# A two-group streaming encoder layer on one core: the layer-input gate's weight sums beside the first projection, the feed-forward operands in another order, the first residual rows requested early

## The chip, the cores and the metric

The kernel runs on one core of one Trainium2 chip. The metric is the device time of one execution in microseconds (us). A core has a matrix engine (TensorE, PE in the profile), three elementwise engines (VectorE is DVE, ScalarE is ACT, GpSimd is POOL) and SyncE (SP), which here issues all transfers, in order, to one queue that 16 DMA engines work off. Each engine runs its instructions in the order in which they stand, and waits on semaphores for the others.

## What is computed

One encoder layer over 1024 prompt tokens and 8 x 16 sample tokens, that is nine tiles of 128 tokens, of width 1024, all in float32:

```python
h = rmsnorm(x, g_mix)
q_a, k_a, v_a, q_b, k_b, v_b = split_heads(h, w_in)      # 1024 -> 3072
a   = stick_breaking(q_a, k_a, v_a, ...)                 # group A, 8 heads; samples also see a cache
o_b = band_attention(q_b, k_b, v_b, ..., rel_table)      # group B, 8 heads
x = x + concat(rmsnorm(a), rmsnorm(o_b)) @ w_out
h = rmsnorm(x, g_ffn)
x = x + (silu(h @ w_gate) * (h @ w_up)) @ w_down         # 1024 -> 2816 -> 1024
gate = sigmoid(rmsnorm(x, g_ple) @ w_ple_gate)           # 1024 x 1024, the layer-input gate
x = x + gate * (p @ w_ple_proj)
y = rmsnorm(x, g_final)
```

The new keys and values are outputs too. In the gate, the scale `g_ple` belongs to the rows of `w_ple_gate`, so that `g_ple * w_ple_gate` depends on weights alone and can be made at any time before the gate's product.

## The kernel before, in words

**Precision and products.** Each float32 operand is split into a high part (a cast on ACT, line L159, L233 or L1303) and the rest (a subtraction, L105, on DVE or POOL), and each product is three matmuls (`mm3`, L100 to L102). The products of the feed-forward block, of the down projection and of the gate use a scheme of Strassen's kind: seven products of half-size blocks instead of eight. Their operands are sums of blocks, `B11, B21, B22, T1, T2, T3, T4` for the feed-forward block ("forms", 16 KB a partition each, both parts together). The gate's weight sums are `gated[0]` to `gated[6]`, written to device memory and read back by the gate's stage at the end.

**Stages.** First projection with normalization (up to about 330 us), attention, output projection and feed-forward norm (ending about 880 us), gate and up products (to about 1350 us), down projection (1350 to 1580 us), gate and end.

**Who sets the order.** A scheduler orders the instructions of each engine, except within `manual_schedule` blocks and `keep_in_program_order`, where they stay as written. `advance(main, side, ratio, steps)` takes steps from a generator `main` and, by `ratio`, takes steps from a generator `side` between them, so that the side's instructions are written down among the main's. Memory comes from pools on the left and on the right end of a partition; a pool that lies where an earlier one was waits for the last users of what was there.

**First projection.** `qkv` works through `w_in` in chunks of 256 columns (`wraw`, 1 MB a load): the keys of group A (0,1,0) and (0,1,1), then its queries (0,0,0) and (0,0,1), then the rest. Keys: nine matmul tiles of 128x256 a chunk go to `st`, are transposed in threes, split into `sq` (two buffers, `tag="sq"`) and stored in device memory (`kT0h`, `kT0l`, L242). Queries: six tiles of 128x384 a chunk, computed already transposed into two PSUM banks (`ps["o"]`), split from the bank by ACT (L236) and DVE (L237) into the same `sq`, and stored (`qT0h`, `qT0l`). A bank is free when both have read it; an `sq` is free when its stores have landed. `draw` loads rows of the key cache for the attention, and `sk` is the first attention load.

**Gate-up to down.** The forms lie in a row in the order in which they are made, T4, B22, B11, B21, T2, T3, T1, after `h8`. When the last product is done, the down stage's pools lie over them: `sA` (`acth`, `actl`, operands of the down products) over the first two, `sB` (`actr` activations, `wr` weights, `sr` sums) over the others. The last gate-up products read T4, then B22. `raws` loads the first operands, `forms` makes them, `put` splits one. `onto` (L1349) adds each product to the residual rows `x1`, which `fetch_x1` (L1363) loads from `x1d`.

**Down stage.** Five rounds (`d`); in rounds 1 to 4 `gate_sums(d - 1)` makes a quarter of the gate's weight sums: four loads of `w_ple_gate` (L1384, 256 KB each), four scalings on ACT (L1385), four subtractions on POOL (L1393 to L1396) and seven stores (L1389, 256 KB each). Its tiles `q00, q01, q10, q11, t2, t3` have one buffer each.

Of the kernel before, what the change touches and what calls it, by code (L numbers as in the profile page):

```python
# [22 lines left out]
P = 128  # L23
D = 1024
KT = 8
NP = 8
NT = 9
# [12 lines left out]
def tile_hymba_step(  # L40
# [37 lines left out]
    nc = tc.nc  # L78
    V, A, G, T = nc.vector, nc.scalar, nc.gpsimd, nc.tensor
# [141 lines left out]
    gated = [dram.tile([P, 4, 512], F32, name=f"gated{i}") for i in range(7)]  # L221
# [496 lines left out]
    left, right = ExitStack(), ExitStack()  # L718
    ps = {}

    def pool(stack, name, side, bufs=1):
        return stack.enter_context(tc.tile_pool(name=name, bufs=bufs, side=side, reuse_waits="tile"))

    def banks(stack, side, **n):
        for k, m in n.items():
            ps[k] = stack.enter_context(
                tc.tile_pool(name=f"ps_{k}_{len(pool_names)}", bufs=m, space=PSUM, side=side, reuse_waits="tile")
            )
            pool_names.append(k)
# [3 lines left out]
    def advance(main, side, ratio, steps=None):  # L733

        due, n = 0.0, 0
        while steps is None or n < steps:
            if next(main, "end") == "end":
                break
            n += 1
            due += ratio  # L740
            while due >= 1.0:
                due -= 1.0
                next(side, None)
        return n
# [12 lines left out]
    with tc.tile_pool(name="x1", bufs=2, side="right") as xp, tc.manual_schedule(engines=all_engines):  # L757
# [22 lines left out]
        for i in range(4):  # L780
            o = slice(i * 2, i * 2 + 2)
# [7 lines left out]
        for t in range(2, NT):  # L789
# [2 lines left out]
            transposed(ps["t"], rows.pop(0), hT, t)  # L792
            next(project)
    start.close()
    banks(first, "left", t=2, s=1)
    advance(project, None, 0, 36 - (NT - 1))

    for i, g in enumerate((g_out_sb, g_out_cb)):
        nc.sync.dma_start(g_out[:, i * 4 : i * 4 + 4], g.rearrange("o (k p) -> p (o k)", p=P))
# [172 lines left out]
    def form(name):  # L972
        return [fp.tile([P, KT // 2, 512], F32R, name=name + n) for n in "hl"]


    h8 = [fp.tile([P, KT, P], F32R, name="h8" + n) for n in "hl"]
    T4, B22, B11, B21, T2, T3, T1 = [form(n) for n in ("T4", "B22", "B11", "B21", "T2", "T3", "T1")]
    g_row = load_row(xg, g_ffn[0:1, :], "grow")

    def gate_up(i):  # L980
# [170 lines left out]
    with tc.tile_pool(name="ph4b", bufs=2, side="right", reuse_waits="tile") as p4b:  # L1151
# [12 lines left out]
        for i in range(n_chunk):  # L1164
# [28 lines left out]
            d = bank()  # L1193
# [60 lines left out]
        bstack = ExitStack()  # L1254
# [105 lines left out]
    def fetch_x1(ts, half):  # L1360
        for t in ts:
            o = slice(half * 512, half * 512 + 512)
            nc.sync.dma_start(x1[t][:, o], x1d[t * P : (t + 1) * P, o])  # L1363


    with tc.manual_schedule(engines={mybir.EngineType.SP}):
        fetch_x1((0, 1, 2, 3, 8), 0)
        fetch_x1((4, 5, 6, 7), 1)
        fetch_x1((0, 1, 2, 3, 8), 1)
        fetch_x1((4, 5, 6, 7), 0)  # L1370
        ahead = raws(1)

    wq = pool(bstack, "wq", "left")
    g_gate = wq.tile([P, KT], F32, name="g_gate")
    nc.sync.dma_start(g_gate, g_ple.rearrange("o (k p) -> p (o k)", p=P))

    def gate_sums(k):

        q = {}
        for x in range(2):  # L1380
            for y in range(2):
                q[x, y] = wq.tile([P, 512], F32, name=f"q{x}{y}", tag=f"q{x}{y}", bufs=1)
                row = (x * 4 + k) * P
                nc.sync.dma_start(q[x, y], w_ple_gate[0, row : row + P, y * 512 : y * 512 + 512])  # L1384
                A.activation(q[x, y], q[x, y], AF.Copy, scale=g_gate[:, x * 4 + k : x * 4 + k + 1])  # L1385
        t2, t3 = [wq.tile([P, 512], F32, name=nm, tag=nm, bufs=1) for nm in ("t2", "t3")]

        def out(i, v):
            nc.sync.dma_start(gated[i][:, k], v)  # L1389

        for i, v in ((0, q[0, 0]), (1, q[1, 0]), (6, q[1, 1])):
            out(i, v)
        G.tensor_tensor(t3, q[1, 1], q[0, 1], op=ALU.subtract)  # L1393
        G.tensor_tensor(q[0, 1], q[0, 1], q[0, 0], op=ALU.subtract)
        G.tensor_tensor(t2, q[1, 1], q[0, 1], op=ALU.subtract)
        G.tensor_tensor(q[1, 0], q[1, 0], t2, op=ALU.subtract)  # L1396
        for i, v in ((2, t2), (3, t3), (4, q[0, 1]), (5, q[1, 0])):
            out(i, v)

    for d in range(nd):  # L1400
        if d:
            ahead = raws(d + 1) if d + 1 < nd else None
        if ahead is None:
            w_last = sB.tile([P, 2, D], F32, name="wr", tag="wr", bufs=3)
            nc.sync.dma_start(w_last, w_down[0, 2 * nd * 256 :, :].rearrange("(f p) c -> p f c", p=P))
            a_last = []
            for f in range(2):
                a_last.append(sB.tile([P, 2, NT * P], F32, name="actr", tag="actr", bufs=4)[:, 0])
                nc.sync.dma_start(a_last[f], actd[2 * nd][:, f])
        A2, W21, A1, W11, d8 = got  # L1410
        got = next(now)
        for m in range(4):
            b = bank()
            times(b, A2, W21, m)
            onto(m, 0, b)
        m1 = []
        for m in range(4):
            m1.append(tbank())
            times(m1[m], A1, W11, m)
            onto(m, 0, m1[m])  # L1420
        b = bank()
        last_tile(d8, 1, W21, b, True, False)
        last_tile(d8, 0, W11, b, False, True)
        onto(NP, 0, b)
        S2, T2, S1, T1 = got
        got = next(now)
        for m in range(4):
            times(m1[m], S2, T2, m, True)
            if d == 0:
                A.copy(u2[m], m1[m])  # L1430
            else:
                V.tensor_tensor(u2[m], u2[m], m1[m], op=ALU.add)
        m5 = []
        for m in range(4):
            m5.append(bank())
            times(m5[m], S1, T1, m)
            onto(4 + m, 1, m5[m])
        S4, W22, W12 = got
        got = next(now)
        for m in range(4):  # L1440
            times(m5[m], S4, W22, m, True)
            onto(m, 1, m5[m])
        b = bank()
        last_tile(d8, 1, W22, b, True, False)
        last_tile(d8, 0, W12, b, False, True)
        onto(NP, 1, b)
        S3, T3, A4, T4 = got
        if d:
            gate_sums(d - 1)
        if ahead is not None:  # L1450
            now = forms(ahead)
            got = next(now)
        else:
            w_d = ch.parts(w_last, 2, D, 2, V)
            act = []
            for f in range(2):
                hl = act_place(NT * P)
                A.copy(hl[0], a_last[f])
                sub(G, hl[1], a_last[f], hl[0])
                act.append(hl)  # L1460
        m7 = []
        for m in range(4):
            m7.append(tbank())
            times(m7[m], S3, T3, m)
            onto(4 + m, 1, m7[m])
        for m in range(4):
            times(m7[m], A4, T4, m, True)
            onto(4 + m, 0, m7[m])
# [270 lines left out]
```

## Time and profile before

| | |
|---|---|
| median of the runs shown | 1710.83 us (1707.01, 1710.83, 1711.6) |
| profiled execution, its time | 1708.87 us |
| its span in the trace | 1707.0 us (1.87 us lie around it) |
| granted TensorE clock | 0.989 |
| PE busy | 1650.5 us, 97% of the span |
| DVE, ACT, POOL busy | 1083.7, 814.2, 819.5 us |
| moved by DMA | 293.50 MB, 172 GB/s on average |

A time in the rows that follow counts from the start of the span. A row of a timeline has the start, the duration, the engine and line, what is written and read, and in brackets how long the engine had been idle and what ended that. In a row of a tile there are minimum, median and maximum durations in ns. In a row by stretches of time the busy time of each engine stands with the number of its instructions, then the granted clock, the share of time that the DMA engines were busy and GB/s.

### The profile page before, as it was taken

To read this page: it belongs to the slowest core of one execution; us is meant where nothing else is said; L and a number is where in the kernel's file an instruction comes from. 1 tells how busy PE (TensorE), PEld (TensorE's weight loads), DVE (VectorE), ACT (ScalarE), POOL (GpSimd) and SP (SyncE) were. 2 spreads that over 40 slices of the span, in tenths; PEclk is the share of its full clock that TensorE was granted. 3 is DMA by queue.
4 is the path that set the end of the run, shared out by engine and by line. 5 is a ranking of instruction groups with operands and counts; after the bars stand their busy time and mean duration, and the time that the engine had idled before them with its cause. 6 is when DMAs were issued, how large, how long until landed. Compare 5 with 4: busy or idle time off the path is not lost.

```text
span 1707.0 us, 27775 instructions
## 1 busy us (share of the span) xinstructions
PE 1650.5 (97%) x10308; PEld 1422.1 (83%) x10308; DVE 1083.7 (63%) x1702; ACT 814.2 (48%) x1724; POOL 819.5 (48%) x666
## 2 busy tenths in 40 slices
PE   8999999989998999898999999999999999999998
PEld 7998888989996887787878888888888788788887
DVE  6111544369889766754677566666655597798875
ACT  5223545367777877643663333333333244433673
POOL 2313311277356511322565555555555378958763
PEclk9999999999998999999999999999999999999999
DMA  5846888656469985955422222222222697712222
GB/s 193 277 151 218 276 292 296 186 179 173 123 175 275 290 262 163 254 173 173 148 87 96 96 96 96 96 96 96 85 86 89 217 384 255 251 67 114 97 99 100
DMA packets 172810, 293.50 MB, mean 172 GB/s; under 512 B 16641, under 2 KB 96257, under 8 KB 170370
## 3 DMA queue, kind: packets, MB, share of 16 engines
q1 hardware_dynamic: 172674, 291.71, 52.1%
q8 instruction: 82, 1.34, 0.3%
q14 instruction: 54, 0.44, 0.1%
HBM read 204.77 MB, written 86.90 MB: 171 GB/s over the span
## 4 chain that ended last, share of the span: by engine, by line
PE 80%; DVE 6%; DMA 6%; ACT 3%; POOL 3%; issue 2%; SPq 1%; POOLq 0%; DVEq 0%; ACTq 0%
PE ps L1076 25%; PE ps L100 7%; PE ps L101 6%; PE ps L102 6%; PE pt L1344 4%; PE pt L1076 4%; PE ps L1344 3%; PE pt L610 2%; PE pt L405 2%; PE acc L468 2%; DMA v<-sv 2%; DVE keep L114 2%; PE sdec L427 1%; PE po L634 1%; PE S L579 1%
## 5 line engine op out<-in xcount | busy, mean ns | idle before, releaser
L105 POOL TENSOR_TENSOR wlo<-wraw,whi 128x512 fp32r<-128x512 f32 (+1 forms) x123 | 216.4, 1783 | 137.9 <-ACT whi L159 137.9
L100 PE MATMUL ps<-whi,hTh 128*128 128x256 f32 x576 | 168.0, 292 | 1.4 <-ACT st L267 1.4
L101 PE MATMUL ps<-wlo,hTh 128*128 128x256 f32 x576 | 164.5, 286 | 0.0
L102 PE MATMUL ps<-whi,hTl 128*128 128x256 f32 x576 | 164.0, 285 | 0.0
L159 ACT CAST whi<-wraw 128x512 fp32r<-128x512 f32 (+1 forms) x122 | 88.6, 743 | 72.5 <-PE ps L1076 27.5
L100 PEld LDWEIGHTS ps<-whi,hTh 128*128 128x128 f32 x576 | 110.6, 192 | 8.0 <-issue 5.7
L592 POOL TENSOR_TENSOR w<-w,keep 128x127 f32<-128x127 f32 (+4 forms) x64 | 78.5, 1229 | 74.8 <-DVE keep L114 64.6
L102 PEld LDWEIGHTS ps<-whi,hTl 128*128 128x128 f32 x576 | 110.7, 192 | 0.6 <-DVE hTl L105 0.2
L101 PEld LDWEIGHTS ps<-wlo,hTh 128*128 128x128 f32 x576 | 110.8, 192 | 0.2
L614 ACT CAST wth<-pt 128x512 fp32r<-128x512 f32 (+1 forms) x192 | 84.3, 466 | 44.1 <-PE pt L610 43.4
L105 DVE TENSOR_TENSOR wtl<-pt,wth 128x512 fp32r<-128x512 f32 (+1 forms) x192 | 94.1, 512 | 14.8 <-ACT wth L614 14.7
L114 DVE TENSOR_TENSOR_SCAN keep<-keep,zero 128x128 f32<-128x128 f32 (+7 forms) x64 | 101.6, 1588 | 1.7
L610 PE MATMUL pt<-ident,w 128*128 128x128 f32 x528 | 90.1, 284 | 6.7 <-DVE wtl L105 3.1
L610 PEld LDWEIGHTS pt<-ident,w 128*128 128x128 f32 x528 | 63.9, 144 | 20.3 <-DVE wtl L105 5.3
L579 PE MATMUL S<-qk 128*128 128x384 f32 (+2 forms) x192 | 71.9, 376 | 7.3 <-ACT keep L583 5.4
L633 PE MATMUL po<-wth,vk 128*128 128x256 f32 (+1 forms) x304 | 76.8, 284 | 1.2 <-DVE wtl L105 1.2
L105 POOL TENSOR_TENSOR actl<-actr,acth 128x1024 fp32r<-128x1024 f32 (+1 forms) x22 | 60.5, 2751 | 32.2 <-DMA sr<-acts 20.7
L634 PE MATMUL po<-wtl,vk 128*128 128x256 f32 (+1 forms) x304 | 73.5, 285 | 0.0
L406 DVE COPY kT<-pt 128x512 f32<-128x512 f32 x48 | 33.0, 687 | 51.7 <-PE pt L405 47.7
L101 PE MATMUL ps<-hTl,whi 128*128 128x384 f32 x192 | 65.4, 341 | 0.0
L102 PE MATMUL ps<-hTh,wlo 128*128 128x384 f32 x192 | 65.3, 340 | 0.0
L100 PE MATMUL ps<-hTh,whi 128*128 128x384 f32 x192 | 65.2, 339 | 0.0
(448 smaller groups left out, 5291.5 us busy)
## 6 DMA issues: line engine op xcount, KB each, us to landing
draw<-in_cache_sb_k SPq DMA_DIRECT2D x32, 512.0 KB, 6.3
draw<-in_cache_sb_v SPq DMA_DIRECT2D x32, 512.0 KB, 5.5
act<-sg SPq DMA_DIRECT2D x11, 1152.0 KB
actr<-act SPq DMA_DIRECT2D x22, 576.0 KB, 6.3
wraw<-in_w_in SPq DMA_DIRECT2D x11, 1024.0 KB, 9.4
wraw<-in_w_gate SPq DMA_DIRECT2D x11, 1024.0 KB, 5.3
wraw<-in_w_up SPq DMA_DIRECT2D x11, 1024.0 KB, 6.3
v<-sv SPq DMA_DIRECT2D x36, 256.0 KB, 4.5
```

Of the source, the lines that this page charges most:

```text
L100: T.matmul(out, lhsT=ah, rhs=bh, start=start, stop=False)
L101: T.matmul(out, lhsT=ah, rhs=bl, start=False, stop=False)
L102: T.matmul(out, lhsT=al, rhs=bh, start=False, stop=stop)
L105: return eng.tensor_tensor(out, a, hi.bitcast(F32), op=ALU.subtract)
L114: V.tensor_tensor_scan(rev, rev, zero[:, 0:1].to_broadcast([P, n - d]), keep[:, n - d : n - d + 1], op0=ALU.mult, op1=ALU.max)
L159: A.copy(h[:, o], v[:, o])
L579: T.matmul(sc, lhsT=hd["qq"][:, qs], rhs=hd["kkh"][:, kc], start=True, stop=False)
L610: T.transpose(pt[:, (c - c0) * P : (c - c0 + 1) * P], w[:, c * P : (c + 1) * P], ident)
L614: A.copy(wth[:, ks, qs], pv)
L634: T.matmul(dst, lhsT=vs, rhs=wtl[:, kb - base, c0:c1], start=False, stop=(i == nkb - 1))
L1076: T.matmul(out, lhsT=a[x][:, k], rhs=b[y][:, k], start=(not more and k == 0 and n == 0), stop=(k == 3 and n == 2), skip_group_check=more)
L1344: T.matmul(out, lhsT=a[i][:, x, m * P : (m + 1) * P], rhs=b[j][:, x], start=(not more and x == 0 and n == 0), stop=(x == 1 and n == 2), sk ...
```

## The change

It has three parts.

1. `gate_sums` moves from the down stage to the first projection. It becomes a generator with three steps a quarter (loads; scalings, three stores and a subtraction; three subtractions and four stores), runs as `side` of `advance` with a ratio of 0.5, and its tiles come from a pool on the right end of memory, with two buffers each, in the place that the input rows `x` leave. The 16 loads, 16 scalings, 16 subtractions and 28 stores are the same ones.
2. The forms are laid out as B21, T2, B11, T3, T1, T4, B22. `sA` then lies over B21 and T2, and `sB` over the others, of which T4 and B22 are the last.
3. `fetch_x1` for the first halves of rows 0 to 3 is called ahead of the `manual_schedule` block rather than within it.

```diff
@@ after the first tiles of the projection
     start.close()
+    qstack = ExitStack()
+    wq = pool(qstack, "wq", "right", 2)
+    g_gate = wq.tile([P, KT], F32, name="g_gate", bufs=1)
+    nc.sync.dma_start(g_gate, g_ple.rearrange("o (k p) -> p (o k)", p=P))
+
+    def gate_sums(k):
+        q = {}
+        for x in range(2):
+            for y in range(2):
+                q[x, y] = wq.tile([P, 512], F32, name=f"q{x}{y}", tag=f"q{x}{y}")
+                row = (x * 4 + k) * P
+                nc.sync.dma_start(q[x, y], w_ple_gate[0, row : row + P, y * 512 : y * 512 + 512])
+        yield
+        for x, y in q:
+            A.activation(q[x, y], q[x, y], AF.Copy, scale=g_gate[:, x * 4 + k : x * 4 + k + 1])
+        t2, t3 = [wq.tile([P, 512], F32, name=nm, tag=nm) for nm in ("t2", "t3")]
...
+        for i, v in ((0, q[0, 0]), (1, q[1, 0]), (6, q[1, 1])):
+            out(i, v)
+        G.tensor_tensor(t3, q[1, 1], q[0, 1], op=ALU.subtract)
+        yield
+        G.tensor_tensor(q[0, 1], q[0, 1], q[0, 0], op=ALU.subtract)
+        G.tensor_tensor(t2, q[1, 1], q[0, 1], op=ALU.subtract)
+        G.tensor_tensor(q[1, 0], q[1, 0], t2, op=ALU.subtract)
+        for i, v in ((2, t2), (3, t3), (4, q[0, 1]), (5, q[1, 0])):
+            out(i, v)
+        yield
+
     banks(first, "left", t=2, s=1)
-    advance(project, None, 0, 36 - (NT - 1))
+    gate_weights = (x for k in range(4) for x in gate_sums(k))
+    advance(project, gate_weights, 0.5, 36 - (NT - 1))
+    for _ in gate_weights:
+        pass
+    qstack.close()
@@ feed-forward
-    T4, B22, B11, B21, T2, T3, T1 = [form(n) for n in ("T4", "B22", "B11", "B21", "T2", "T3", "T1")]
+    B21, T2, B11, T3, T1, T4, B22 = [form(n) for n in ("B21", "T2", "B11", "T3", "T1", "T4", "B22")]
@@ down
+    fetch_x1((0, 1, 2, 3), 0)
     with tc.manual_schedule(engines={mybir.EngineType.SP}):
-        fetch_x1((0, 1, 2, 3, 8), 0)
+        fetch_x1((8,), 0)
...
-    wq = pool(bstack, "wq", "left")
...
-        if d:
-            gate_sums(d - 1)
```

**The first projection, SP's queue at the change from keys to queries.** Before, from the last four key stores on (names as in the code, with buffer numbers; `sq_980` and `sq_1027` are the same buffer of two):

```order
L242 DMA kT0h_72<-sq_980 128x384
L242 DMA kT0h_72<-sq_989 128x384
L242 DMA kT0l_73<-sq_980 128x384
L242 DMA kT0l_73<-sq_989 128x384
L141 DMA wraw_1182<-in_w_in 128x8x256
L365 DMA sk0_1621<-kT0h_72 128x4x128
L242 DMA qT0h_70<-sq_1027 128x384
L242 DMA qT0l_71<-sq_1027 128x384
```

The same place now (`sq_1028` is what was `sq_980`, `wraw_1255` what was `wraw_1182`; L814 are the stores and L807 the loads of `gate_sums`):

```order
L141 DMA wraw_1255<-in_w_in 128x8x256
L814 DMA gated3_116<-t3_1250 128x512
L807 DMA q10_1392<-in_w_ple_gate 128x512
L814 DMA gated0_113<-q00_1388 128x512
L814 DMA gated4_117<-q01_1179 128x512
L814 DMA gated6_119<-q11_1394 128x512
L814 DMA gated2_115<-t2_1249 128x512
L814 DMA gated1_114<-q10_1181 128x512
L242 DMA kT0h_72<-sq_1028 128x384
L242 DMA kT0l_73<-sq_1028 128x384
L242 DMA kT0h_72<-sq_1037 128x384
L814 DMA gated3_116<-t3_1461 128x512
```

The load of the next weights and seven transfers of `gate_sums` now stand ahead of the first of the last four key stores. The loads `draw`, which stood earlier, now stand behind the first four query stores.

**The same place on POOL and ACT.** POOL now has, from the split of the chunk before on:

```order
L105 TENSOR_TENSOR wlo_193<-wraw_1044,whi_192 128x1024 x2
L818 TENSOR_TENSOR t3_1250<-q11_1183,q01_1179 128x512
L820 TENSOR_TENSOR q01_1179<-q01_1179,q00_1177 128x512
L821 TENSOR_TENSOR t2_1249<-q11_1183,q01_1179 128x512
L818 TENSOR_TENSOR t3_1461<-q11_1394,q01_1390 128x512
```

ACT now has, up to the first query split (before, L233, L233 and L236 stood side by side):

```order
L233 CAST sq_1028<-pt_1024 128x384
L810 ACTIVATE q01_1390<-q01_1390,g_gate_646 128x512
L233 CAST sq_1037<-pt_1033 128x384
L810 ACTIVATE q10_1392<-q10_1392,g_gate_646 128x512
L236 ACTIVATE sq_1075<-ps_1050 128x384
```

Two scalings have come between the splits, and on POOL the four subtractions of a quarter follow the split of `wraw_1044`, where nothing stood before.

**The down stage, POOL in the round that starts about 1450 us.** Before:

```order
L1310 TENSOR_TENSOR t2_15411<-wraw_15133,t2_15411 128x1024
L1393 TENSOR_TENSOR t3_16059<-q11_16055,q01_16049 128x512
L105 TENSOR_TENSOR actl_15584<-sr_15149,acth_15583 128x1024
L1394 TENSOR_TENSOR q01_16049<-q01_16049,q00_16046 128x512
L105 TENSOR_TENSOR actl_15653<-actr_15138,acth_15652 128x1024
L1395 TENSOR_TENSOR t2_16058<-q11_16055,q01_16049 128x512
L1310 TENSOR_TENSOR wr_15141<-wraw_15133,wr_15141 128x2x512
L1396 TENSOR_TENSOR q10_16052<-q10_16052,t2_16058 128x512
```

The same place now:

```order
L1346 TENSOR_TENSOR t2_15487<-wraw_15234,t2_15487 128x1024
L105 TENSOR_TENSOR actl_15660<-sr_15250,acth_15659 128x1024
L105 TENSOR_TENSOR actl_15729<-actr_15239,acth_15728 128x1024
L1346 TENSOR_TENSOR wr_15242<-wraw_15234,wr_15242 128x2x512
L105 TENSOR_TENSOR actl_15735<-actr_15236,acth_15734 128x1024
```

The subtractions are gone from between the splits.

**SP at the start of down.** The rows here read as before but for line numbers and buffer numbers: the last activations, then the residual rows 0 to 3 and 8:

```order
L1285 DMA act10_100<-sg_14540 128x2304
L1399 DMA x1_0_14885<-x1d_89 128x512
L1399 DMA x1_1_14886<-x1d_89 128x512
L1399 DMA x1_2_14887<-x1d_89 128x512
L1399 DMA x1_3_14888<-x1d_89 128x512
L1399 DMA x1_8_14893<-x1d_89 128x512
```

Nothing has moved past anything in this stretch of the queue.

More of the change, by code (lines that the diff above doesn't have):

```diff
@@ L794, in tile_hymba_step, with out @@
     start.close()
-    banks(first, "left", t=2, s=1)
-    advance(project, None, 0, 36 - (NT - 1))
+    qstack = ExitStack()
[13 more added lines that the diff above has]
+        t2, t3 = [wq.tile([P, 512], F32, name=nm, tag=nm) for nm in ("t2", "t3")]
+        def out(i, v):
+            nc.sync.dma_start(gated[i][:, k], v)
+        for i, v in ((0, q[0, 0]), (1, q[1, 0]), (6, q[1, 1])):
[8 more added lines that the diff above has]
+        yield
+    banks(first, "left", t=2, s=1)
+    gate_weights = (x for k in range(4) for x in gate_sums(k))
[3 more added lines that the diff above has]
+    qstack.close()
     for i, g in enumerate((g_out_sb, g_out_cb)):
@@ L1371, in tile_hymba_step @@
         ahead = raws(1)
-    wq = pool(bstack, "wq", "left")
[L1374 to L1398, printed above, removed]
     for d in range(nd):
```

## The prediction

> **What bounds the kernel now.** I read the page's busy shares and its chain first, then the stretches of time, then the waits of PE, and last the timelines of the two places that the change touches.
>
> ```profile
> PE 1650.5 (97%) x10308; PEld 1422.1 (83%) x10308; DVE 1083.7 (63%) x1702; ACT 814.2 (48%) x1724; POOL 819.5 (48%) x666
> PE 80%; DVE 6%; DMA 6%; ACT 3%; POOL 3%; issue 2%; SPq 1%; POOLq 0%; DVEq 0%; ACTq 0%
> ```
>
> PE is busy for 97% and makes 80% of the chain. Work moved between the other engines is therefore worth only what PE waits for it, and whatever makes PE wait is lost for good. So I compare PE at the place that loses work with PE at the place that gets it.
>
> ```profile
> 80.00:100.00 20.00, 20.00 (x118) 19.97 (x117) 3.81 (x7) 3.35 (x8) 1.00 (x1) 1.00 0.59 195
> 1340.00:1360.00 20.00, 19.23 (x86) 15.54 (x86) 11.80 (x10) 6.88 (x9) 7.60 (x4) 1.00 0.71 253
> 1360.00:1380.00 20.00, 19.16 (x84) 15.28 (x83) 18.50 (x19) 8.26 (x10) 18.84 (x7) 1.00 1.00 376
> 1460.00:1480.00 20.00, 18.55 (x82) 15.02 (x81) 11.80 (x15) 9.65 (x12) 18.68 (x10) 1.00 0.91 319
> 1480.00:1500.00 20.00, 19.71 (x84) 15.13 (x83) 20.00 (x21) 5.96 (x7) 18.97 (x9) 1.00 0.46 169
> 1500.00:1520.00 20.00, 20.00 (x90) 16.54 (x89) 18.71 (x21) 7.11 (x8) 11.62 (x5) 1.00 0.32 112
> ```
>
> In the first projection (80 to 100 us) PE has no gap, and DVE, ACT and POOL are nearly idle: room on the engines, none on PE. In down a full stretch of 20 us holds 90 matmuls (1500 to 1520), one per 0.222 us. The four other stretches hold 86, 84, 82 and 84, so 24 are missing, 24 x 0.222 = 5.3 us. That is the most that the transition and the down stage together can give back. PE's waits from 1340 to 1500 us name part of it:
>
> ```profile
> PE pt L1344 <- ACT whi L1303: 1.4, 1, 1.4
> PE ps L100 <- DVE x L1349: 0.8, 1, 0.8
> PE ps L1344 <- POOL actl L105: 0.8, 1, 0.8
> ```
>
> **Part 1a, the sums leave down.** What one quarter does there:
>
> ```profile
> L1385 ACT ACTIVATE q<-q,g_gate x16: 706/724/727, 1398.5 to 1485.1; 128x512 f32<-128x512 f32 x16
> L1393 POOL TENSOR_TENSOR t<-q,q x4: 1284/1294/1310, 1410.9 to 1473.7; 128x512 f32<-128x512 f32 x4
> L1394 POOL TENSOR_TENSOR q<-q,q x4: 2270/2275/2290, 1415.5 to 1477.3; 128x512 f32<-128x512 f32 x4
> L1395 POOL TENSOR_TENSOR t<-q,q x4: 1284/1302/2262, 1420.1 to 1479.7; 128x512 f32<-128x512 f32 x4
> L1396 POOL TENSOR_TENSOR q<-q,t x4: 1260/1783/2280, 1424.7 to 1490.1; 128x512 f32<-128x512 f32 x4
> ```
>
> ACT is rid of 16 x 0.724 = 11.6 us, POOL of 4 x (1.294 + 2.275 + 1.302 + 1.783) = 26.6 us, SP of 44 transfers of 256 KB. Nearly all of it ran beside PE. What lay on the path shows in the chain around 1465 us (start, duration, what):
>
> ```profile
> 1459.66 2.28 POOL q L1394
> 1464.26 1.28 POOL t L1395
> 1465.54 2.37 POOL wr L1310
> 1467.93 1.05 ACT whi L1303
> 1469.01 1.24 DVE wlo L105
> ```
>
> PE's wait of 1.4 us is for `whi`, which waits for POOL's `wr`, which stood behind two subtractions of `q`, 2.28 + 1.28 = 3.6 us in all. Without them `wr` is ready over 2 us earlier and the wait goes; with the pipeline's refill it is 8 missing matmuls from 1460 to 1480, 1.8 us. After it DVE has no pause (20.00 of 20.00 us from 1480 to 1500) and PE lacks 6 more, 1.3 us; DVE got its late start from the same chain, so I count most of that, 1.1. Sum: 2.9 us. The bounds are 1.4 (the named wait alone) and 3.1 (all 14 matmuls). What would be late next is `wr<-in_w_down`, but with 44 transfers fewer in the queue it lands sooner, not later.
>
> **Part 1b, the sums enter the first projection.** ACT, DVE and POOL have room. SP's queue and POOL's order matter, at the change from keys to queries. Before:
>
> ```profile
> 76.25 4.75 POOL L105 TENSOR_TENSOR wlo<-wraw,whi 128x1024 fp32r<-128x1024 f32 x2 [8.82 <-ACT whi L159]
> 80.88 0.80 SPq L242 DMA_DIRECT2D kT0h<-sq  x2
> 81.77 0.89 SPq L242 DMA_DIRECT2D kT0l<-sq  x2
> 82.76 0.41 SPq L141 DMA_DIRECT2D wraw<-in_w_in  x1
> 85.03 0.33 SPq L242 DMA_DIRECT2D qT0l<-sq  x1
> 83.92 0.49 ACT L236 ACTIVATE sq<-ps 128x384 fp32r<-128x384 f32 x1 [2.68 <-DMA kT0l<-sq]
> 84.44 0.56 DVE L237 SCALAR_TENSOR_TENSOR sq<-ps,sq 128x384 fp32r<-128x384 f32 x1 [2.54 <-ACT sq L236]
> 85.54 0.49 ACT L236 ACTIVATE sq<-ps 128x384 fp32r<-128x384 f32 x1 [1.13 <-PE ps L102]
> DMA to landing us min/median/max: 1.8/1.9/7.0
> ```
>
> The first query tile is ready at 83.92 - 2.68 = 81.24, but ACT must wait until `kT0l` has landed and freed an `sq`. DVE is done with the bank at 85.00. The second tile ends at about 85.4 (ACT takes it at 85.54), and then PE needs the first bank again: it has 0.4 us to spare. The last row is the landing time of the `qT0l` stores in this projection: 1.9 us with a free queue, 7.0 behind the weight load of 82.76.
>
> Now the key store that frees that `sq` stands behind the weight load, seven transfers of the sums and, by way of `gated2<-t2`, three subtractions on POOL that come after the split of 76.25. That split ends at 81.00. The least delay: POOL 81.00 + 3 x 1.29 = 84.9, then SP's issues of `gated2`, `gated1`, `kT0h` and `kT0l` at 0.33 each, 86.2, landing 1.9, 88.1, ACT 0.49 and DVE 0.56, 89.2. PE restarts at 89.2 rather than 85.4: 3.8 us. The most: `kT0l` lands behind everything issued from 81.3 on, 1024 KB of weights, 7 x 256 KB and 2 x 192 KB, 3.2 MB. At 376 GB/s (the row 1360 to 1380, DMA busy all the time) this takes 8.7 us, to 90.0; at the 320 GB/s of the row 1460 to 1480 it takes 10.2, to 91.5. With about 1.4 us of landing beyond the transfer (1.9 less the store's own half microsecond) and 1.05 for ACT and DVE, PE restarts at 92.4 to 94.0: 7.0 to 8.6 us. I take 7.0, since the queue showed the same thing on a smaller scale: one 1 MB load made a landing of 1.9 into 7.0.
>
> The Trainium skill (DMA: Bandwidth & Descriptors, section "Queues, rings and completion order") says that on each DMA engine descriptors are taken in ring order, yet completion is not first-in first-out for the issuing engine. By completions that overtake, the store would land as with a free queue, the stall would be 3.8 and the sum +0.9. The landing of 7.0 behind the weight load speaks for the ring's order.
>
> After the stall the second query bank has a whole tile of matmuls (24 x 0.174, 4.2 us) before PE wants it, and the `draw` loads behind the first query stores are first needed in the attention, some 50 us later. I cost them at nothing; if that cover is gone, one more landing behind 3 x 512 KB costs 1.5 MB / 376, 4 us less the tile's 4.2. Earlier in this projection I find no wait that the new work lengthens beyond its slack.
>
> **Part 2, the order of the forms.**
>
> ```profile
> 1330.28 11.67 SPq L1260 DMA_DIRECT2D actr<-act  x4
> 1342.00 0.43 SPq L1268 DMA_DIRECT2D wr<-in_w_down  x1
> 1343.66 4.46 SPq L1274 DMA_DIRECT2D sr<-acts  x6
> 1352.40 2.39 POOL L105 TENSOR_TENSOR actl<-actr,acth 128x1024 fp32r<-128x1024 f32 x1 [20.75 <-DMA sr<-acts]
> 1354.85 0.50 PE L1344 MATMUL ps<-whi,actl 128*128 128x512 f32 x1 [0.77 <-POOL actl L105]
> 1356.94 3.42 DVE L1310 TENSOR_TENSOR t<-wr 128x1024 f32<-128x1024 f32 x1
> 1364.32 1.27 DVE L1349 TENSOR_TENSOR x<-x,ps 128x512 f32<-128x512 f32 x2
> ```
>
> POOL's first `actl` starts at 1352.40, just as the last gate-up product is through: the release is put down to a transfer long landed, but `actl` lay over B22, which that product reads. With B21 and T2 there instead, `acth` and `actl` can start right after the loads, over 2 us earlier, and PE's 0.77 (0.9 with refill) goes. In return, the second half of `actr`, `wr` and `sr` now lie over T3, T1, T4 and B22, the last ones read, and the issue of `wr` moves from 1342 to about 1347. `wr` then lands near 1355, the split to `wlo` is done near 1358.4, and PE needs it at 1357.5 to 1358. So a wait of 0.8 goes and one of up to 0.9 comes, and DVE's `t` (3.42) and with it the `x` of 1364.32 may slip by half a microsecond. Together between -1.1 and +1.5; I take 0.
>
> **Part 3, the residual rows.** SP's order there is word for word what it was; they stay behind the stores of the last activations. Zero.
>
> **Sum.** +7.0 - 2.9 + 0 + 0 = +4.1 us. Against the profiled execution, 1708.9 + 4.1 = 1713.0 us. That execution lies 2.0 us under the median shown, so that from the median it would be 1714.9; the difference is within the spread of the three runs. 0.3% of this kernel, about what a measurement can tell from no change, is 5.1 us. My forecast is no difference by that bound, with the sign towards slower.
>
> **The rivals.**
>
> A, the key stores are not held back as computed: POOL's subtractions or the landing take less, and the stall lies between nothing and 3.8. For it speaks that 3.8 is the least only if POOL begins after 81.0. Against it, the split before them waits for ACT's `whi`, hence for PE, and was there at 76.25 for that reason. The time is 1708.9 - 2.9 = 1706.0 with no stall, down to 1703.6 with all of the 5.3 recovered, and 1709.8 with 3.8.
>
> B, slower: the stall at the change from keys to queries is 8.2 us or more. It decides where `kT0l` lands after 92.6 (93.6 on PE, less 1.05). For it speak the 320 GB/s, and that the load before 92.07, when `qT0l` of 85.03 landed, drained slower still: 1024 KB, `sk`'s 256 and two or three stores took from 82.76 until then. Price: 8.6 to 11, less 2.9, or +5.7 to +8.1, 1714.6 to 1717.0.
>
> C, down gives nothing back: the wait at 1469 turns into one for another operand, since 20 of 20 us of DVE from 1480 on say that DVE is the bound there. Then +7.0, and with a lengthened transition +8.5: 1715.9 to 1717.4. Against it speaks that the wait's own chain runs through the subtractions.
>
> D, POOL's subtractions also slow DVE in down. The splits there show it:
>
> ```profile
> L105 DVE TENSOR_TENSOR wlo<-t,whi x12: 1211/1962/2899, 1366.1 to 1514.9; 128x1024 fp32r<-128x1024 f32 x12
> ```
>
> The same instruction takes 1.21 us or up to 2.90. If what POOL gives up (26.6 us) comes back to DVE, all of the 5.3 is recovered: +7.0 - 5.3 = +1.7, 1710.6 us. Against it: the longest of them come beside `actl`, which stays. The Trainium skill (SBUF — State Buffer, section "SBUF: two separate sides") has a rule for it: VectorE with two SBUF inputs and GpSimd hold one port pair exclusively, and the loser waits for the whole instruction. The trace agrees with a wait of that size (2.90 less 1.21), and the rule would give the sum of this rival; in the first projection the splits of DVE read one operand from PSUM, so that by the same rule nothing is lost there.
>
> **How the numbers follow.** The forecast (+4.1, 1711 to 1715) 0.32; A 0.20, half of it below -5.1 us or near enough to be told as faster; B 0.21 and C 0.12, both slower by over 0.3%; D 0.15, no difference. Faster 0.10, same 0.32 + 0.15 + 0.10 = 0.57, slower 0.33. The range leaves out half of A below and the end of B above: 1706 to 1718.
>
> **What would show it.** In the changed trace: a wait of PE at 85 to 94 us, 4 to 9 us long, put down to DVE or ACT behind ACT's L236, which waits for `kT0l`; no stall before it; PE's wait for `whi` near 1469 gone, and 88 to 90 matmuls in each 20 us from 1460 to 1500; the wait for `actl` at 1354 gone, another of under 1 us near 1358; `x1` rows issued at the same place as before. The prediction is wrong if PE has no gap at 85 us, or has further ones in the projection, or if the gaps in down stay without the subtractions.

## The result: 16 us slower, and the profile after

The changed kernel takes 1727.31 us (median of 6 runs, 1722.19 to 1729.53), the kernel before 1711.21 us (6 runs, 1707.01 to 1714.72). The ratio is 1.0083, with a 95% interval of 1.0068 to 1.0098: slower by 16 us, beyond the 1718 of the range. The profiled execution took 1728.58 us with a span of 1726.8.

The busy shares, the chain and the stretches of the changed kernel, as they were shown of before (the same place comes about 15 us later from the queries on and 20 to 23 us later in down):

```profile
PE 1654.0 (96%) x10308; PEld 1428.3 (83%) x10308; DVE 1080.2 (63%) x1702; ACT 816.5 (47%) x1724; POOL 802.8 (46%) x666
PE 81%; DMA 6%; DVE 5%; ACT 4%; POOL 2%; issue 2%; SPq 0%; POOLq 0%; ACTq 0%; DVEq 0%
60.00:80.00 20.00, 20.00 (x162) 20.00 (x161) 3.04 (x6) 8.59 (x16) 12.67 (x9) 1.00 1.04 373
80.00:100.00 20.00, 7.02 (x40) 6.63 (x39) 1.70 (x4) 5.50 (x9) 10.28 (x8) 0.76 1.03 372
100.00:120.00 20.00, 20.00 (x106) 20.00 (x106) 2.31 (x5) 4.08 (x6) 4.96 (x7) 0.90 0.94 308
1380.00:1400.00 20.00, 15.76 (x63) 12.59 (x62) 16.06 (x17) 7.19 (x9) 12.99 (x6) 0.91 1.00 371
1480.00:1500.00 20.00, 20.00 (x90) 16.57 (x89) 15.96 (x18) 6.23 (x6) 9.82 (x5) 1.00 0.67 237
1500.00:1520.00 20.00, 20.00 (x90) 16.57 (x89) 19.08 (x22) 7.79 (x9) 11.66 (x6) 1.00 0.16 53
```

Two rows of the projection before:

```profile
60.00:80.00 20.00, 20.00 (x162) 20.00 (x161) 2.92 (x6) 7.09 (x12) 8.51 (x4) 1.00 0.72 247
100.00:120.00 20.00, 20.00 (x117) 20.00 (x116) 2.79 (x5) 4.43 (x7) 4.74 (x2) 1.00 0.41 141
```

Two stretches show the loss. From 80 to 100 us PE is busy for 7.02 us where it had been busy for 20, and its granted clock is 0.76 there and 0.90 in the next stretch, where PE has no pause but makes 106 matmuls instead of 117. From 1380 to 1400 it lacks 4.2 us, again with a lower clock. The stretches that had lacked matmuls in down now have 90 each. PE's waits in the first projection and in down are one each:

```profile
PE ps L100 <- DVE sq L237: 13.0, 1, 13.0
PE ps L100 <- DVE x L1385: 4.2, 1, 4.2
```

By lining up PE's instructions of the two traces one by one, the delay of the changed kernel against before (at times of before) reads: 0.4 us at 80 us, 16.0 from 110 to 140, 15.5 from 160 to 330, behind the first projection's keys and queries, 19.2 from 880 to 1340, 22.9 from 1380 to 1455, 19.8 from 1505 to the end. So +15.5 in the projection, +3.7 at the start of down, -3.1 in the rest of down: +16.1, as much as the medians differ. The other 3.7 us arise between 330 and 880, where the change edits nothing, and are not shown to belong to it: a second trace of the changed kernel has 1.0 us there. The reading differs from execution to execution: in two kernels below that change nothing ahead of 1350 (the forms' order alone, the sums early in down) it moves from 160 us on between 0.1 and 4.8 us and stands at 2.9 and at 0.5 us from 880 on. The profiled execution of before also lies 2.3 us under its median, and that of the changed kernel 1.3 us over its own.

Where the 13 us come from, in SP's and ACT's timelines of the changed kernel, with the longest of SP's own waits from 76 to 100 us and the landing times of the `kT0l` stores from 60 to 100 us (minimum, median, maximum):

```profile
81.69 0.32 SPq L242 DMA_DIRECT2D kT0l<-sq  x1
83.73 0.32 SPq L242 DMA_DIRECT2D kT0l<-sq  x1
84.27 0.38 SPq L141 DMA_DIRECT2D wraw<-in_w_in  x1
89.76 0.45 SPq L814 DMA_DIRECT2D gated<-q  x1
92.35 0.32 SPq L242 DMA_DIRECT2D kT0h<-sq  x1
93.02 0.32 SPq L242 DMA_DIRECT2D kT0l<-sq  x1
86.49 0.48 ACT L233 CAST sq<-pt 128x384 fp32r<-128x384 f32 x1 [1.47 <-DMA kT0l<-sq]
93.64 0.72 ACT L810 ACTIVATE q<-q,g_gate 128x512 f32<-128x512 f32 x1 [5.18 <-DMA q<-in_w_ple_gate]
97.77 0.49 ACT L236 ACTIVATE sq<-ps 128x384 fp32r<-128x384 f32 x1 [3.41 <-DMA kT0l<-sq]
SPq L242 <- DMA wraw<-in_w_in: 2.1, 1, 2.1
DMA to landing us min/median/max: 4.4/4.7/7.9
```

Of before, the split of the last keys and the landing times of the `kT0l` stores from 38 to 112 us:

```profile
80.37 0.86 ACT L233 CAST sq<-pt 128x384 fp32r<-128x384 f32 x2 [2.53 <-PE pt L273]
DMA to landing us min/median/max: 1.9/2.0/2.2
```

It is the chain that the prediction named, but it starts earlier. The `kT0l` stores ahead of the last two are issued at 81.69 and 83.73, behind transfers of the sums, and the first lands 4.7 us later; only then can ACT split the last keys, at 86.49 instead of 80.37. (One step further back it is the same: a `kT0l` store of 68.06 took 7.9 us to land.) Then come `wraw` and the sums' transfers, as computed. SP reaches the last key stores at 92.35, after a wait of 2.1 us that is put down to the landing of `wraw`; why a store waits for that load, the views do not show. The store of 93.02 lands just before 97.77; the first query split follows there instead of at 83.92, and PE restarts at 98.91 instead of 85.4.

### The profile page after: what moved, and what is told of

It reads as the page before. It is cut to its first block, busy times and chain, and to the rows that moved or that the text cites. A ratio compares the mean times of both kernels' runs of the same rounds, so it can differ in the third digit from the quotient of the medians.

```text
span 1726.8 us, 27792 instructions
## 1 busy us (share of the span) xinstructions
PE 1654.0 (96%) x10308; PEld 1428.3 (83%) x10308; DVE 1080.2 (63%) x1702; ACT 816.5 (47%) x1724; POOL 802.8 (46%) x666
## 4 chain that ended last, share of the span: by engine, by line
PE 81%; DMA 6%; DVE 5%; ACT 4%; POOL 2%; issue 2%; SPq 0%; POOLq 0%; ACTq 0%; DVEq 0%
PE ps L1112 25%; PE ps L100 7%; PE ps L101 6%; PE ps L102 6%; PE pt L1380 6%; PE ps L1380 4%; PE pt L1112 3%; PE pt L610 2%; PE pt L405 2%; DMA v<-sv 2%; PE acc L468 1%; PE po L634 1%; PE sdec L427 1%; PE S L579 1%; DVE keep L114 1%
## 5 line engine op out<-in xcount | busy, mean ns | idle before, releaser
L105 DVE TENSOR_TENSOR wtl<-pt,wth 128x512 fp32r<-128x512 f32 (+1 forms) x192 | 94.0, 512 | 14.9 <-ACT wth L614 14.6
L105 POOL TENSOR_TENSOR actl<-actr,acth 128x1024 fp32r<-128x1024 f32 (+1 forms) x22 | 54.6, 2484 | 45.8 <-ACT acth L1339 43.2
```

Of the source, the lines that this page charges most:

```text
L105: return eng.tensor_tensor(out, a, hi.bitcast(F32), op=ALU.subtract)
```

## The experiments

My theory after the result: (1) in the projection the sums' transfers fill the queue, so that key stores land late and PE waits 13 us, and the clock falls in that wait; (2) the forms' order makes the wait at the start of down longer; (3) the residual rows' edit does nothing; (4) down gains 2.9 us without the sums. The rivals are in the expectations.

**Part 1 alone, part 2 alone.** In the first, the forms and the residual rows are as before; in the second, only this line differs from before:

```diff
-    T4, B22, B11, B21, T2, T3, T1 = [form(n) for n in ("T4", "B22", "B11", "B21", "T2", "T3", "T1")]
+    B21, T2, B11, T3, T1, T4, B22 = [form(n) for n in ("B21", "T2", "B11", "T3", "T1", "T4", "B22")]
```

> The kernel before with part 1 alone (the gate's weight sums beside the first projection; forms and residual rows as before). My theory: the loss of the change is the wait of PE between the second and the third query tile (13.1 us) and the lower granted clock behind it (2.4), 15.5 in all, and down gives back 2.9: +12.6 us, about 1723.5. Rival: the sums also cost something outside of these two places, or the forms cost nothing: then part 1 alone costs what the whole change does, +16, about 1727.

> The kernel before with part 2 alone (the forms laid out as B21, T2, B11, T3, T1, T4, B22). My theory: the wait for actl at the start of down goes (-1.3), and the operands that are requested 5 us later put the store of the last activations and the residual rows behind 3.7 MB, so that PE waits 4.2 us for the first sum onto a residual row and runs at half clock for 4 us after it (+4.5): +3.2 us, about 1714. Rival: the long wait comes from the sums' absence or from another state of the queue, and the order of the forms by itself costs nothing: 1711, with a wait of about 1 us there.

Part 1 alone: 1723.20 us against 1711.91, ratio 1.0069 (1.0046 to 1.0092), that is +11.3; PE waits 13.7 us at the same place. Part 2 alone: 1713.46, ratio 1.0006 (0.9995 to 1.0017), not told from before. In its trace the wait for `actl` is gone, and the one for the residual row is 1.9 us instead of 0.8:

```profile
PE ps L100 <- DVE x L1349: 1.9, 1, 1.9
PE pt L1344 <- ACT whi L1303: 1.8, 1, 1.8
```

So part 1 carries the loss, and the forms' order alone is the zero that was predicted. Together with part 1 it costs 3.7 us at the start of down in the changed kernel's trace. The row of PE's delay for part 1 alone also falls by 2.9 us in down (17.5 to 14.6).

**Part 3 taken out again, and the changed kernel once more.** The first is the changed kernel with `fetch_x1((0, 1, 2, 3, 8), 0)` back in the manual block.

> The changed kernel without part 3: the residual rows 0 to 3 are fetched within the manual block again. Open is why the wait for the first sum onto a residual row is 4.2 us in the changed kernel and 1.9 with the forms' order alone. My theory: part 3 does nothing (SP's order is the same), and the wait is a matter of a landing near 1380 that comes 1 us later and of DVE beside POOL; so this kernel has a wait of 2 to 4.4 us there and takes what the changed one takes, about 1727. Rival: part 3 causes the longer wait; then it is 1.9 here, and the time is 3 to 4 us shorter, 1723.

> The changed kernel once more. With its order of the forms the wait for the first sum onto a residual row was 4.2 us in three traces and 1.8 to 1.9 in two, with part 3 and without it. Theory chance: the wait depends on a landing that varies between executions of one kernel; 1.8 or 4.2 here, and the clock falls after the longer one. Rival: it is fixed by the program, and is 4.2 again within 0.1.

Without part 3: 1727.83 us, ratio 1.0076 (1.0058 to 1.0094), the same as the changed kernel, with the same wait (4.2 us). Part 3 does nothing. The changed kernel in a second trace (one run, 1729.59 us) waited 4.4 us. That speaks against "chance": with the sums moved and the forms reordered the wait was 4.2 to 4.4 in four traces without added matmuls. But it does not settle it: a fifth trace, of the kernel with matmuls added near 90 us (below), has the same code in down and waited 1.8 there, so that the order of down's instructions alone does not fix the wait. The rows of DVE at that place, of part 2 alone and then of the changed kernel:

```profile
1365.79 1.48 DVE L1310 TENSOR_TENSOR t<-wraw,t 128x1024 f32<-128x1024 f32 x1 [4.21 <-DMA act<-sg]
1367.20 1.27 DVE L1349 TENSOR_TENSOR x<-x,ps 128x512 f32<-128x512 f32 x2
```
```profile
1383.22 2.73 DVE L1346 TENSOR_TENSOR t<-wraw,t 128x1024 f32<-128x1024 f32 x1 [5.26 <-DMA act<-sg]
1385.87 1.27 DVE L1385 TENSOR_TENSOR x<-x,ps 128x512 f32<-128x512 f32 x2
```

The longer wait has two halves: the store of the last activations lands 1.05 us later (DVE waited 5.26 rather than 4.21), and the subtraction behind it takes 2.73 rather than 1.48 us beside POOL's `actl` (which runs there in part 2 alone too, so that it depends on where the two instructions meet). The Trainium skill (SBUF — State Buffer, "SBUF: two separate sides") has VectorE with two SBUF inputs and GpSimd exclude each other for whole instructions; a `t` that takes 1.25 us longer agrees with that. Why the store lands 1 us later with the same order in SP's queue stays open.

**A third order of the forms**, `T4, T1, B11, B21, T2, T3, B22`, in the kernel before:

> The kernel before with the forms laid out as T4, T1, B11, B21, T2, T3, B22, which only swaps B22 and T1: the low parts of the first activations then lie over T1, read 6 us earlier than B22, and only two of the six loads of sums lie over B22. My theory: the wait for actl (0.9) goes, and with no more than 1 MB requested late the residual rows come as before: -0.5 to -0.9, about 1710.5, told from before only by the trace. Rival: any of the late requests pushes the residual rows, and the wait for them grows from 1.0 to 2 or more: no gain or +1.

1712.95 us, ratio 1.0002 (0.9992 to 1.0012). The wait for `actl` went, the one for the residual row grew to 2.7 us: the rival. By SP's order, whatever lies over the last form read is requested late, and the residual rows stand behind it.

**The key stores in ACT's own queue.** In the changed kernel:

```diff
+            queue = nc.scalar if (grp, w) == (0, 1) else nc.sync
             for x in range(2):
-                nc.sync.dma_start(qkT[grp][w][x][c, :, g * 384 : (g + 1) * 384], hl[x])
+                queue.dma_start(qkT[grp][w][x][c, :, g * 384 : (g + 1) * 384], hl[x])
```

> The changed kernel, with the stores of group A's keys issued by ACT into its own queue instead of by SP. The sums' transfers are the same ones, at the same time. My theory: what held the key stores was SP's order (wraw and the sums' transfers ahead of them, each waiting for its data). With that gone the wait between the second and the third query tile falls from 13 us to under 2 and the clock stays up: 1711 + 3.2 - 2.9 + 0 to 2, about 1712 to 1714. Rival: the DMA engines are simply full at that time (busy over 1.0 from 60 to 100 us), and the stores take as long through any queue: a wait of 5 us or more, 1718 or above.

1736.90 us, ratio 1.0134 (1.0114 to 1.0154): the worst of all. There are now waits before the queries as well, since ACT stands still until a store may be issued, and the copies that free PE's banks stand behind that:

```profile
PE ps L100 <- DVE sq L237: 8.2, 2, 7.1
PE pt L274 <- ACT st L268: 6.1, 2, 4.2
```

The wait at the queries is still 7.1 us, though no transfer of the sums stands ahead of the key stores in their queue. So "SP's order" was only half of the theory. The engines were full (busy 0.99 there), and the last key store took 6.9 us to land. The Trainium skill (DMA: Bandwidth & Descriptors, "Issuing engines are not separate DMA queues") says that transfers from several engines run on the same 16 DMA engines and interleave; this run agrees.

**Half of the sums.** Two quarters in the projection, two in rounds 1 and 2 of down, forms and residual rows as before:

> Part 1 with two quarters of the sums beside the first projection and two in down, in rounds 1 and 2. Here no transfer of the sums stands ahead of the last four key stores, but five loads of the key cache do (draw, 2.5 MB), which the scheduler has put there. It tells whether the sums' own order matters or the bytes in the queue. Theory bytes: a load of 2.5 MB needs some 7 us, so a wait of 3 to 8 us between the second and the third query tile, with a lower clock where it is over 4: 1713 to 1719. Theory order (a store held by data that is not there yet): the loads wait for nothing, no stall: about 1709 to 1711.

1719.99 us, ratio 1.0034 (1.0021 to 1.0046); PE's wait at the queries is 8.1 us. No transfer of the sums stands there, but loads of the key cache that wait for nothing, and the splits wait as before:

```profile
78.27 2.87 SPq L141 DMA_DIRECT2D draw<-in_cache_sb_k  x5
86.80 0.38 SPq L242 DMA_DIRECT2D kT0l<-sq  x1
92.65 0.49 ACT L236 ACTIVATE sq<-ps 128x384 fp32r<-128x384 f32 x1 [10.05 <-DMA kT0l<-sq]
```

Bytes in the queue are enough; the sums' own dependences need not be involved.

**Sums and weights held behind the key stores.** The scheduler orders SP's queue by itself, so a dependency is used. In part 1 alone:

```diff
-                nc.sync.dma_start(q[x, y], w_ple_gate[0, row : row + P, y * 512 : y * 512 + 512])
+                with tc.issue_after(out_marks[-1].ins) if k > 1 else ExitStack():
+                    nc.sync.dma_start(q[x, y], w_ple_gate[0, row : row + P, y * 512 : y * 512 + 512])
...
-    advance(project, gate_weights, 0.5, 36 - (NT - 1))
+    advance(project, gate_weights, 0.75, 8)
+    advance(project, None, 0, 4)
+    advance(project, gate_weights, 0.75, 28 - 12)
```

where `out_marks` has the key and query stores traced so far. The next run adds the same for the load of weights in (0,0,0), and the last one for the scalings on ACT (with one step more between loads and scalings of the later quarters, and a last ratio of 1.0):

```diff
-            load(i + 1)
+            with tc.issue_after(out_marks[-1].ins) if (grp, w, c) == (0, 0, 0) else ExitStack():
+                load(i + 1)
...
```

> Part 1 alone, with the loads of the third and fourth quarter of the sums held behind the stores of the second query tile in SP's queue (a dependency, since the scheduler orders SP by itself). Ahead of the last four key stores then stands the weight load, but no transfer of the sums. My theory: the wait between the second and the third query tile falls from 13.7 us to under 1, the clock stays up, and what down gives back remains: -2 to -3 us against before, about 1709. Rival: the DMA engines have too little left (the sums need 31 us of them, and between 85 and 140 us they were idle for some 28), so that the loads for the attention come late and a wait of 3 us or more appears at 140 to 180 us: no gain or slower.

> As in the run before with two quarters held (part 1 alone, the third and fourth quarter's loads behind the stores of the second query tile), and the next load of weights (1 MB) held behind the last key stores too. That run still had a wait of 4.2 us between the second and the third query tile, with no transfer of the sums ahead of the key stores, only the weight load. My theory: the key stores waited behind that 1 MB and what was left of earlier transfers; with it behind them the wait falls to under 1 us and the clock stays at 1.0, and down's gain remains: -2 to -3 us against before. Rival: the queue is still full from 60 to 80 us with the first two quarters, so that the stores land late all the same: a wait of 2 us or more, and no gain.

> As in the run before (part 1 alone, half the sums' loads and the next weights held behind stores), with ACT's scalings of the third and fourth quarter also held behind a later query split, two tiles after their loads. In that run ACT stood before two scalings whose loads had not landed, and the query splits behind them came late: PE waited 1.0 and 1.5 us. My theory: these two waits go, nothing else changes, and what down gives back (2.9) is left: -2 to -3 us against before, 0.9985. Rival: the loads of the key cache, which the scheduler puts behind the sums, come late for the attention, and a wait of 2 us or more appears from 140 to 180: no gain.

With the loads held: 1714.30 us, ratio 1.0013 (1.0000 to 1.0025). The wait is down from 13.7 to 4.2 us; `kT0l` stood behind `wraw` alone. With the weights held too: 1711.79, ratio 0.9991 (0.9981 to 1.0001). ACT's first query split now comes as in the kernel before, and PE has no gap there; two waits of 1.0 and 1.5 us come later, where ACT stands before scalings whose loads have not landed:

```profile
84.26 0.49 ACT L238 ACTIVATE sq<-ps 128x384 fp32r<-128x384 f32 x1 [2.68 <-DMA kT0l<-sq]
122.99 2.03 ACT L814 ACTIVATE q<-q,g_gate 128x512 f32<-128x512 f32 x3 [3.83 <-DMA q<-in_w_ple_gate]
```

With the scalings held as well these two are gone, and waits at the start of the attention are longer, where before had 2.8 and 0.2 us:

```profile
PE pt L408 <- DVE kT L409: 3.2, 1, 3.2
PE pt L408 <- ACT kT L409: 2.1, 1, 2.1
```

The key cache's loads, the rival of the expectation, do not explain the second one: those ahead of it are issued by 137.1 us and landed by 143, and PE first reads them at 150.4. ACT, which has to copy the bank out, had four copies of `qbd` and a cast ahead of that copy; that this order makes the wait was not tested.

1711.00 us, ratio 0.9989 (0.9977 to 1.0001): the fastest here, 1.6 us below the median of before on the same chip, but its interval just reaches 1. In the three traces PE's delay falls by 2.7 to 3.2 us in down, about as in the changed kernel.

**The sums left in down, two quarters in round 1 and two in round 2:**

```diff
-        if d:
-            gate_sums(d - 1)
+        if d in (1, 2):
+            gate_sums(2 * d - 2)
+            gate_sums(2 * d - 1)
```

> The kernel before with the sums left in down, but two quarters each in rounds 1 and 2 rather than one each in rounds 1 to 4. It tells whether down's waits at 1469 and later hang on the subtractions that stand in POOL's order in those rounds. My theory: they do; rounds 3 and 4 then have none, PE's wait for whi at 1469 and the slower stretch to 1495 go, while rounds 1 and 2 have no tight place (90 matmuls in each 20 us from 1380 to 1460): -2 to -3 us, about 1709 to 1711. Rival: twice the transfers and subtractions in a round make new waits in rounds 1 and 2 (the DMA engines are busy for 0.64 to 1.04 there): no gain or slower.

1715.40 us, ratio 1.0012 (1.0003 to 1.0021): slower by 0.1%. A new wait of 2.8 us stands at 1458, and that for `whi` stays:

```profile
PE pt L1344 <- DVE x L1349: 3.7, 3, 2.8
PE pt L1344 <- ACT whi L1303: 1.3, 1, 1.3
```

But this run does not tell whether that wait hangs on the subtractions, for the edit did not move them: each tile has one buffer, and in its trace they run from 1411.4 to 1495.4 us, where before had them from 1410.9 to 1490.1. Two stand ahead of `wr` again:

```profile
1464.65 2.28 POOL L1394 TENSOR_TENSOR q<-q,q 128x512 f32<-128x512 f32 x1
1469.26 1.28 POOL L1395 TENSOR_TENSOR t<-q,q 128x512 f32<-128x512 f32 x1
1470.51 2.39 POOL L1310 TENSOR_TENSOR wr<-wraw,wr 128x1024 f32<-128x1024 f32 x1
```

The run with half of the sums tells it. There the eight subtractions that are left in down are over at 1461.7, none stands in the 14 us ahead of that `wr`, the wait for `whi` is gone, and PE's delay falls from 14.2 to 11.2 us; this is its row by stretches:

```profile
1460.00:1480.00 20.00, 20.00 (x90) 16.53 (x90) 19.39 (x21) 8.48 (x9) 17.02 (x8) 1.00 0.43 144
```

So the wait goes when the later rounds are rid of the sums, and two quarters in rounds 1 and 2 make no wait of over 0.8 us.

**PE kept busy in its wait.** 66 matmuls more between the second and the third query tile of the changed kernel:

```diff
+                if (grp, c) == (0, 0) and (pr, g) == (0, 2):
+                    warm = ps["t"].tile([P, 384], F32, name="warm", tag="T")
+                    for n in range(66):
+                        x = T.matmul(warm, lhsT=wh[:, 0, m], rhs=hT.rows(0, 0)[0], start=True, stop=True, skip_group_check=True)
+                        tc.keep_in_program_order(x)
...
```

> The changed kernel with 66 matmuls of 128x384 more (11.5 us at 0.174) into an unused PSUM bank, between the second and the third query tile, where PE waits for 13 us. Their result is not used. My theory: the idle PE costs a second time, since the clock granted after the wait is 0.5 for some 6 us; with PE kept busy the third tile starts at the same time, at full clock, and everything behind it comes 2.4 us earlier than in the changed kernel: a shift of 13.1 rather than 15.5 us against before at 140 us. Rival: the clock falls for another reason, or the slow start is a warm-up of the tiles' operands: the shift at 140 us stays 15.5 or grows.

Inconclusive on the total: PE's delay from 110 to 140 us is 15.3 us against 16.0, since the added matmuls themselves ran at half clock at first and so outlasted the wait. (The time, 1724.40 us from two runs, ratio 1.0062 with 1.0041 to 1.0084, also has a wait of only 1.8 us at the start of down.) What it shows is the clock. First the changed kernel (us, PE busy, ..., granted clock, DMA share, GB/s), then this one:

```profile
88.00:90.00 2.00, 0.00 (x0) 0.00 (x0) 0.56 (x1) 0.47 (x1) 1.92 (x2) 1.00 1.02 309
90.00:98.90 8.90, 0.00 (x0) 0.00 (x0) 0.56 (x1) 1.21 (x2) 2.83 (x3) 0.52 1.05 399
98.90:104.00 5.10, 5.09 (x16) 5.09 (x17) 0.56 (x1) 0.49 (x1) 2.03 (x5) 0.50 0.75 269
104.00:108.00 4.00, 4.00 (x25) 4.00 (x24) 0.56 (x1) 0.49 (x1) 0.00 (x0) 1.00 1.02 212
```
```profile
88.00:91.40 3.40, 3.40 (x12) 3.40 (x11) 0.56 (x1) 0.43 (x1) 3.24 (x3) 0.50 1.01 342
91.40:95.00 3.60, 3.60 (x22) 3.60 (x22) 0.00 (x0) 0.45 (x1) 0.27 (x1) 1.00 1.05 395
```

Without work the clock is 0.50 from about 90.4 and stays so for 5.1 us after PE has restarted: about 2.5 us lost, an estimate from half of that time. With work from 87.5 on it is 0.50 for 3.4 us only. So the lower clock follows the idle time and goes with work; that much is shown.

## Why the prediction was wrong, point by point

- **The place and the chain of part 1 were right**: PE's only gap in the projection lies between the second and the third query tile, put down to DVE behind ACT's L236, which waits for `kT0l`.
- **Its size was wrong, and this is the step that failed.** "I take 7.0", with 8.6 as the most. The wait is 13.0 us. The prediction counted the bytes "issued from 81.3 on" and said "Earlier in this projection I find no wait that the new work lengthens beyond its slack". But the DMA engines were already full from 60 us on (share 1.04, 373 GB/s, where before had 0.72), so the key stores before the last ones landed in 4.7 us instead of 2.0, and the last key split came at 86.49 instead of 80.37. The sum began 6 us too early: from the last key split to PE's restart it had 12.0 us, and 12.4 were measured. 7.0 + 6.1 is 13.1.
- **A term was missing**: the granted clock after a long wait of PE, about 2.5 us here. The trace of before could have told: its granted clock is 0.50 from 806 to 810, behind a wait of PE of 4.6 us that ends at 806.7.
- **The same term makes part 2 dear.** Its bounds were -1.1 to +1.5 with 0 taken. Alone it measured 1.0006 (0.9995 to 1.0017), so 0 was right for it alone. With part 1 it was +3.7 in the changed kernel's trace, outside the bounds: 4.2 us of wait and half clock for 3.4 us. "May slip by half a microsecond" was the step that failed there; that the two parts do not add was not considered, and why the store lands later stays open.
- **Part 1a, -2.9, was right**: -3.1 in the trace of the changed kernel, -2.9 with part 1 alone and with half of the sums, -2.7 to -3.2 in the three held versions. The wait for `whi` is gone in all of them, as foretold.
- **Part 3, zero, was right.**
- **The rivals.** B (slower by a longer stall) had the sign and 0.21, but its price of +5.7 to +8.1 was half of what came. A, C and D fall: the stall was not shorter, down did give back about 3, and not more.
- The measured sum: +15.5 in the projection (13.0 of wait and about 2.5 of clock), +3.7, -3.1, together +16.1, as between the medians.

## What to carry to other kernels

Work that fills "idle" engines beside a bound stage still shares the transfer queue with the small stores that free that stage's buffers: look for the place with the least slack (here 0.4 us), and count the backlog from the moment at which the DMA engines become full, not from the moment of the store. If such work must go there, hold its transfers, and large loads, behind those stores by a dependency; with that, the same move cost nothing, and what it gained (1.4 to 1.6 us) is not told from nothing. And a wait of the matrix engine of 2 us or more can have a price beyond itself, the slower clock behind it.

## What was not expected of the hardware

The granted clock moves in steps of about 3.4 us: it was 0.50 for 13.6 us in the first wait of the changed kernel (90.4 to 104.0), for 3.4 in the second, and for 3.4 with a gap of 4.2 (loads held) or 1.8 us (matmuls added). After the 1.9 us of part 2 alone it did not fall; after the 1.8 us that the same run waits for `whi` it did, for 3.4 us. The Trainium skill (TensorE: Matmul & The Clock Gate, "What's actually happening") gives a free-running window of 3413 ns and half rate after an idle one. The steps agree; that a window must be idle throughout does not agree with these traces. What decides is the share of one step in which PE worked, as three steps show, first the one ahead of the slower clock with matmuls added, then those with the 1.9 and the 1.8 us of part 2 alone:

```profile
84.58:87.99 3.41, 1.59 (x10) 1.27 (x9) 0.56 (x1) 1.70 (x4) 0.84 (x2) 1.00 0.93 308
1364.14:1367.55 3.41, 1.86 (x9) 1.20 (x7) 1.76 (x2) 1.69 (x2) 3.41 (x2) 1.00 1.04 399
1469.96:1473.37 3.41, 1.63 (x8) 1.03 (x7) 1.15 (x2) 1.75 (x2) 3.41 (x3) 1.00 0.98 344
```

PE worked for 47, 54 and 48% of them, and the clock fell behind the first and the third. Counted over the steps at full clock of all fourteen traces, 119 of the 126 with PE at work for less than half were followed by a step at 0.50, 17 of the 54 with 50 to 62%, and none of the 6596 with more. So a wait costs clock when it takes about half of one such step or more.
